# A softmax streamed through SBUF: late loads in two large tiles, first load on another queue, and one multiply per tile

## The chip, the cores and the metric

The kernel runs on one core of one Trainium2 chip. The metric is device time in microseconds, the median of repeated runs. Lower is better.

## The reference

```python
def reference(x):                 # x: 16 x 1024 x 512, float32
    temp = 2.0
    x_scaled = x / temp
    x_max = np.max(x_scaled, axis=-1, keepdims=True)
    exp_x = np.exp(x_scaled - x_max)
    return exp_x / np.sum(exp_x, axis=-1, keepdims=True)
```

It is a softmax over the last axis with temperature 2. There are 16,384 independent rows of 512 floats; input and output are 33.55 MB each.

## The kernel before

The 16,384 rows are spread over 128 partitions, so that each partition has 128 rows. Below, "a row" means one such row on all 128 partitions: 512 floats by 128 partitions, 262,144 bytes. `PLAN` cuts the 128 rows into tiles; a tile is one load and one store. Each entry holds the tile's chunks (rows per chunk) and the tile's first place in `arena`, an SBUF tensor with room for 100 rows per partition. The tiles have 3, 7, seven times 15, 7, 3 and 3 rows. Everything is done in place in the arena: load, maximum, exponential, multiply, store.

The first eight tiles (0 to 7) fill the 100 rows. Tiles 8 to 11 are late loads: each goes to a place that an earlier tile used, and so has to wait until the stores of those tiles (`behind`) have finished. `AFTER` says after which tile's exponentials ScalarE comes to that wait: late loads are issued from ScalarE's own queue between its exponentials (L133 to L137), so everything behind them on ScalarE waits too.

For each chunk there are four steps:

- VectorE takes the negated maximum of each row with one instruction for the chunk (`do_max`, L100), once the tile's load semaphore `ld` has arrived.
- ScalarE takes the exponential row by row with the maximum as bias, scale 0.5, and sums each row as it goes (L139).
- VectorE takes the reciprocal of the chunk's sums (L109).
- VectorE multiplies the chunk by its reciprocals (`do_mul`). In tiles named in `FUSED` this is one tensor_mul of the whole chunk with the reciprocals broadcast along the row (L113); in all others it is one tensor_scalar_mul for each row (L120).

VectorE's order is written out: the maximum of chunk k, then the multiply of chunk k - `LAG`, with `LAG` = 2. SyncE waits for a tile's last multiply and issues its store (L161). All loads are issued from ScalarE's queue, the first two (`issue_loads(0, 2)`) ahead of a barrier at the start of the program, the others behind it. The second load (`SPREAD`) is issued in three pieces: all rows but one, then the last row over 126 partitions and over 2 partitions. GpSimd waits for all stores at the end.

Of the kernel before, what the change touches and what calls it, by code (L numbers as in the profile page):

```python
# [8 lines left out]


PLAN = [
    ([3], 0), ([4, 3], 3), ([5] * 3, 10), ([5] * 3, 25), ([5] * 3, 40), ([5] * 3, 55),
    ([5] * 3, 70), ([5] * 3, 85), ([5] * 3, 10), ([4, 3], 3), ([3], 0), ([3], 25),
]
ARENA = 100
LAG = 2

AFTER = {8: 4, 9: 4, 10: 4, 11: 6}

SPREAD = 1  # L20

FUSED = {1, 2, 3}


@with_exitstack
def kernel(
    ctx: ExitStack,
    tc: tile.TileContext,
    x: bass.AP,
    out: bass.AP,  # L30
):
    nc = tc.nc
    fp32 = mybir.dt.float32

    xf = x.flatten_outer_dims()
    of = out.flatten_outer_dims()
    N, D = xf.shape
    P = nc.NUM_PARTITIONS
    n_rows = N // P
    assert sum(sum(c) for c, _ in PLAN) == n_rows  # L40

    arena = nc.alloc_sbuf_tensor("arena", (P, ARENA, D), fp32)
    negmax = nc.alloc_sbuf_tensor("negmax", (P, n_rows), fp32)
    sums = nc.alloc_sbuf_tensor("sums", (P, n_rows), fp32)
    recip = nc.alloc_sbuf_tensor("recip", (P, n_rows), fp32)

    tiles, chunks, base = [], [], 0
    for t, (cs, at) in enumerate(PLAN):  # L50
        r = sum(cs)
        tiles.append((base, r, at))
        o = 0
        for c in cs:
            chunks.append((t, base + o, c, at + o))
            o += c
        base += r
    last_chunk = {c[0]: k for k, c in enumerate(chunks)}

    def dram(ap, t):  # L60
        b, r, _ = tiles[t]
        return ap[b * P : (b + r) * P].rearrange("(p r) d -> p r d", r=r)

    def sb(t):
        _, r, at = tiles[t]
        return arena[:, at : at + r, :]


    behind = {}
    for t, (_, r, at) in enumerate(tiles):  # L70
        for u in range(t):
            _, ru, au = tiles[u]
            if at < au + ru and au < at + r:
                behind.setdefault(t, []).append(u)

    ld = [tc.alloc_semaphore(f"ld{t}") for t in range(len(tiles))]
    awaited = sorted({u for us in behind.values() for u in us})
    st = {t: tc.alloc_semaphore(f"st{t}") for t in awaited}
    s_end = tc.alloc_semaphore("s_end")
    s_max = tc.alloc_semaphore("s_max")  # L80
    s_exp = tc.alloc_semaphore("s_exp")
    s_rec = tc.alloc_semaphore("s_rec")
    s_mul = tc.alloc_semaphore("s_mul")

    def issue_loads(begin, end):

        for t in range(begin, end):
            if t == SPREAD:

                r = tiles[t][1] - 1  # L90
                for p, q, lo, hi in ((0, P, 0, r), (0, 126, r, r + 1), (126, P, r, r + 1)):
                    nc.scalar.dma_start(
                        out=sb(t)[p:q, lo:hi], in_=dram(xf, t)[p:q, lo:hi]
                    ).then_inc(ld[t], 16)
            elif t not in behind:
                nc.scalar.dma_start(out=sb(t), in_=dram(xf, t)).then_inc(ld[t], 16)

    def do_max(k):
        t, b, c, a = chunks[k]
        nc.vector.reduce_max(  # L100
            out=negmax[:, b : b + c],
            in_=arena[:, a : a + c],
            axis=mybir.AxisListType.X,
            negate=True,
        )._wait_ge(ld[t], 48 if t == SPREAD else 16).then_inc(s_max, 1)

    def do_mul(k):
        t, b, c, a = chunks[k]
        nc.vector.reciprocal(  # L109
            out=recip[:, b : b + c], in_=sums[:, b : b + c]  # L110
        )._wait_ge(s_exp, k + 1).then_inc(s_rec, 1)
        if t in FUSED:
            nc.vector.tensor_mul(  # L113
                out=arena[:, a : a + c],
                in0=arena[:, a : a + c],
                in1=recip[:, b : b + c].unsqueeze(2).to_broadcast([P, c, D]),
            )._wait_ge(s_rec, k + 1).then_inc(s_mul, 1)
            return
        for r in range(c):
            ins = nc.vector.tensor_scalar_mul(  # L120
                out=arena[:, a + r],
                in0=arena[:, a + r],
                scalar1=recip[:, b + r : b + r + 1],
            )
            if r == 0:
                ins._wait_ge(s_rec, k + 1)
        ins.then_inc(s_mul, 1)

    def compute_and_store():

        late = sorted(behind)
        for k, (t, b, c, a) in enumerate(chunks):
            while late and last_chunk[AFTER[late[0]]] < k:  # L133
                u = late.pop(0)
                for v in behind[u]:
                    nc.scalar.wait_ge(st[v], 16)
                nc.scalar.dma_start(out=sb(u), in_=dram(xf, u)).then_inc(ld[u], 16)  # L137
            for r in range(c):
                ins = nc.scalar.activation(  # L139
                    out=arena[:, a + r],  # L140
                    in_=arena[:, a + r],
                    func=mybir.ActivationFunctionType.Exp,
                    bias=negmax[:, b + r : b + r + 1],
                    scale=0.5,
                    accum_out=sums[:, b + r : b + r + 1],
                )
                if r == 0:
                    ins._wait_ge(s_max, k + 1)
            ins.then_inc(s_exp, 1)


        for k in range(len(chunks) + LAG):
            if k < len(chunks):
                do_max(k)
            if k >= LAG:
                do_mul(k - LAG)


        for t in range(len(tiles)):
            nc.sync.wait_ge(s_mul, last_chunk[t] + 1)  # L160
            nc.sync.dma_start(out=dram(of, t), in_=sb(t)).then_inc(  # L161
                st[t] if t in awaited else s_end, 16
            )

        for t in awaited:
            nc.gpsimd.wait_ge(st[t], 16)
        nc.gpsimd.wait_ge(s_end, 16 * (len(tiles) - len(awaited)))

    hook = nc.inst_callbacks[-1]
    nc.remove_inst_callback(hook)
    symbolic = nc._always_lower_symbolic_ap
    nc._always_lower_symbolic_ap = False
    here = str(nc.cur_bb)
    entry = nc.main_func.blocks[0]
    head, jumps = entry.instructions[:-5], entry.instructions[-5:]
    entry.instructions = []
    nc.switch_bb("main", None)
    issue_loads(0, 2)  # L180
    first = list(entry.instructions)
    at = next(k for k, i in enumerate(head) if type(i).__name__ == "InstDrain")
    entry.instructions = head[:at] + first + head[at:]
    issue_loads(2, len(tiles))
    compute_and_store()
    entry.instructions = list(entry.instructions) + jumps
    nc.switch_bb(here, None)
    nc._always_lower_symbolic_ap = symbolic
    nc.push_inst_callback(hook)
# [30 lines left out]
```

## Time and profile before

| | |
|---|---|
| median of 19 runs | 162.03 us (161.86 to 162.18) |
| the profiled execution | 161.86 us |
| its span in the profile | 160.1 us |
| VectorE (DVE) busy | 131.8 us, 155 instructions |
| ScalarE (ACT) busy | 94.6 us, 257 instructions |
| bytes moved by DMA | 67.14 MB, 419 GB/s over the span |
| maximum, line L100 | 28 instructions, 72.3 us |
| multiply by rows, L120 | 91 instructions, 37.8 us |
| multiply by chunks, L113 | 8 instructions, 21.0 us |

The span reaches from the first instruction to the last DMA packet; the time of an execution has 1.8 us more. In the groups of instructions each row names line, engine, operation, operands with their shapes, and count; behind the first bar stand the busy time in microseconds and the mean of one in nanoseconds, behind the second the idle time of the engine just before them and what ended it. In lines of the timeline the first number is the start and the second the duration, both in microseconds. "q1" is the DMA queue of SyncE and "q10" that of ScalarE in the packet records; each of the 16 DMA engines serves both.

### The profile page before, as it was taken

To read this page: it belongs to the slowest core of one execution; us is meant where nothing else is said; L and a number is where in the kernel's file an instruction comes from. 1 tells how busy PE (TensorE), PEld (TensorE's weight loads), DVE (VectorE), ACT (ScalarE), POOL (GpSimd) and SP (SyncE) were. 2 spreads that over 40 slices of the span, in tenths; PEclk is the share of its full clock that TensorE was granted. 3 is DMA by queue.
4 is the path that set the end of the run, shared out by engine and by line. 5 is a ranking of instruction groups with operands and counts; after the bars stand their busy time and mean duration, and the time that the engine had idled before them with its cause. 6 is when DMAs were issued, how large, how long until landed. Compare 5 with 4: busy or idle time off the path is not lost.

```text
span 160.1 us, 482 instructions
## 1 busy us (share of the span) xinstructions
DVE 131.8 (82%) x155; ACT 94.6 (59%) x257; POOL 0.2 (0%) x4
## 2 busy tenths in 40 slices
DVE  0466499999999999999999999999999999506800
ACT  0629266768449547766688666786667975501300
POOL 0000000000000000000000000000000000000000
DMA  7998999999998989898989999998999999999894
GB/s 279 444 407 384 424 434 421 433 474 376 425 480 384 476 384 484 376 484 378 476 384 476 407 468 422 432 468 380 454 418 451 419 396 431 431 448 468 375 418 204
DMA packets 3603, 67.14 MB, mean 419 GB/s; under 512 B 400, under 2 KB 400, under 8 KB 1296
## 3 DMA queue, kind: packets, MB, share of 16 engines
q10 hardware_dynamic: 1872, 33.56, 49.6%
q1 hardware_dynamic: 1728, 33.56, 48.8%
q14 instruction: 3, 0.02, 0.0%
HBM read 33.55 MB, written 33.55 MB: 419 GB/s over the span
## 4 chain that ended last, share of the span: by engine, by line
DVE 78%; DMA 10%; another core or an unknown queue 5%; issue 0%; DVEq 0%
DVE negmax L100 40%; DVE arena L120 23%; DVE arena L113 13%; DMA arena<-in_x_dram 10%; DVE recip L109 2%; DVEq L215 0%
## 5 line engine op out<-in xcount | busy, mean ns | idle before, releaser
L139 ACT ACTIVATE arena<-arena,negmax 128x512 f32<-128x512 f32 x128 | 90.8, 710 | 49.6 <-DVE negmax L100 49.6
L100 DVE TENSOR_REDUCE negmax<-arena 128x5 f32<-128x2560 f32 (+2 forms) x28 | 72.3, 2585 | 18.7 <-DMA arena<-in_x_dram 18.7
L120 DVE TENSOR_SCALAR arena<-arena,recip 128x512 f32<-128x512 f32 x91 | 37.8, 482 | 0.7
L139 ACT ACTIVATION_READ_ACCUMULATOR arena<-arena,negmax 128x1 f32 x128 | 23.9, 187 | 0.0
L113 DVE TENSOR_TENSOR arena<-arena,recip 128x2560 f32<-128x2560 f32 (+2 forms) x8 | 21.0, 2625 | 0.3
L109 DVE RECIPROCAL recip<-sums 128x5 f32<-128x5 f32 (+2 forms) x28 | 4.9, 176 | 0.0
L139 ACT ACT_TABLE_LOAD x1 | 1.3, 1283 | 5.4 <-issue 5.4
L204 POOL MEMSET const-bfloat16-1.0<- 128x1 bf16 x1 | 0.1, 103 | 0.0
L204 POOL MEMSET const-uint8-127<- 128x1 uint8 x1 | 0.1, 102 | 0.0
L204 POOL MEMSET const-float32-0.0<- 128x1 f32 x1 | 0.1, 100 | 0.2 <-issue 0.2
L204 POOL MEMSET const-float32-1.0<- 128x1 f32 x1 | 0.1, 99 | 0.0
## 6 DMA issues: line engine op xcount, KB each, us to landing
arena<-in_x_dram ACTq DMA_DIRECT2D x7, 3840.0 KB, 42.7
out_dram<-arena SPq DMA_DIRECT2D x7, 3840.0 KB, 23.4
out_dram<-arena SPq DMA_DIRECT2D x2, 1792.0 KB, 12.4
arena<-in_x_dram ACTq DMA_DIRECT2D x3, 768.0 KB, 50.8
out_dram<-arena SPq DMA_DIRECT2D x3, 768.0 KB, 7.5
arena<-in_x_dram ACTq DMA_DIRECT2D x1, 1792.0 KB, 55.6
arena<-in_x_dram ACTq DMA_DIRECT2D x1, 1536.0 KB
arena<-in_x_dram ACTq DMA_DIRECT2D x1, 252.0 KB
```

The costliest lines, as they stand in the source:

```text
L100: nc.vector.reduce_max(out=negmax[:, b : b + c], in_=arena[:, a : a + c], axis=mybir.AxisListType.X, negate=True,)._wait_ge(ld[t], 48 if t ...
L109: nc.vector.reciprocal(out=recip[:, b : b + c], in_=sums[:, b : b + c])._wait_ge(s_exp, k + 1).then_inc(s_rec, 1)
L113: nc.vector.tensor_mul(out=arena[:, a : a + c], in0=arena[:, a : a + c], in1=recip[:, b : b + c].unsqueeze(2).to_broadcast([P, c, D]),)._w ...
L120: ins = nc.vector.tensor_scalar_mul(out=arena[:, a + r], in0=arena[:, a + r], scalar1=recip[:, b + r : b + r + 1],)
L139: ins = nc.scalar.activation(out=arena[:, a + r], in_=arena[:, a + r], func=mybir.ActivationFunctionType.Exp, bias=negmax[:, b + r : b + r ...
L204: nc = _bacc.Bacc("TRN2", target_bir_lowering=False, num_devices=1)
```

## The change

There are now ten tiles instead of twelve: 3, 7, seven times 15, and 13 rows. `PLAN` has a new middle entry, the groups in which a tile is multiplied and stored. A tile of 15 rows has its maxima taken in chunks of 8 and 7 and is multiplied and stored as one group of 15. The late loads are tile 8 (15 rows, at place 0, behind tiles 0, 1 and 2) and tile 9 (13 rows, at place 15, behind tiles 2 and 3); tile 9 has chunks of 5, 4 and 4 and groups of 9 and 4. The first load is issued from SyncE (`FIRST`). Every multiply is one tensor_mul over its group. A group is multiplied once the maxima of the two chunks after its last chunk have been issued, so VectorE's order becomes: the two maxima of tile t, then reciprocal and multiply of tile t - 1. The second load's three pieces are in both kernels. The constants `SPREAD`, `LAG`, `FIRST` and `AFTER` appear twice with the same values.

```diff
 PLAN = [
-    ([3], 0), ([4, 3], 3), ([5] * 3, 10), ([5] * 3, 25), ([5] * 3, 40), ([5] * 3, 55),
-    ([5] * 3, 70), ([5] * 3, 85), ([5] * 3, 10), ([4, 3], 3), ([3], 0), ([3], 25),
+    ([3], [3], 0), ([4, 3], [7], 3), ([8, 7], [15], 10), ([8, 7], [15], 25),
+    ([8, 7], [15], 40), ([8, 7], [15], 55), ([8, 7], [15], 70), ([8, 7], [15], 85),
+    ([8, 7], [15], 0), ([5, 4, 4], [9, 4], 15),
 ]
...
-AFTER = {8: 4, 9: 4, 10: 4, 11: 6}
+FIRST = 1
+AFTER = {8: 4, 9: 6}
...
         for t in range(begin, end):
+            if t in behind:
+                continue
+            queue = nc.sync if t < FIRST else nc.scalar
             if t == SPREAD:
                 r = tiles[t][1] - 1
-                for p, q, lo, hi in ((0, P, 0, r), (0, 126, r, r + 1), (126, P, r, r + 1)):
...
+                parts = (0, P, 0, r), (0, 126, r, r + 1), (126, P, r, r + 1)
+            else:
+                parts = ((0, P, 0, tiles[t][1]),)
+            for p, q, lo, hi in parts:
+                queue.dma_start(
+                    out=sb(t)[p:q, lo:hi], in_=dram(xf, t)[p:q, lo:hi]
+                ).then_inc(ld[t], 16)
...
-    def do_mul(k):
-        t, b, c, a = chunks[k]
+    def do_mul(j):
+        t, b, c, a, k = groups[j]
         nc.vector.reciprocal(
             out=recip[:, b : b + c], in_=sums[:, b : b + c]
-        )._wait_ge(s_exp, k + 1).then_inc(s_rec, 1)
-        if t in FUSED:
...
-        for r in range(c):
-            ins = nc.vector.tensor_scalar_mul(
...
+        )._wait_ge(s_exp, k).then_inc(s_rec, 1)
+        nc.vector.tensor_mul(
+            out=arena[:, a : a + c],
+            in0=arena[:, a : a + c],
+            in1=recip[:, b : b + c].unsqueeze(2).to_broadcast([P, c, D]),
+        )._wait_ge(s_rec, j + 1).then_inc(s_mul, 1)
...
                 for v in behind[u]:
-                    nc.scalar.wait_ge(st[v], 16)
+                    nc.scalar.wait_ge(st[v], 16 * len(PLAN[v][1]))
...
+        j = 0
         for k in range(len(chunks) + LAG):
             if k < len(chunks):
                 do_max(k)
-            if k >= LAG:
-                do_mul(k - LAG)
+            while j < len(groups) and groups[j][4] + LAG <= k + 1:
+                do_mul(j)
+                j += 1
...
-        for t in range(len(tiles)):
-            nc.sync.wait_ge(s_mul, last_chunk[t] + 1)
-            nc.sync.dma_start(out=dram(of, t), in_=sb(t)).then_inc(
+        for j, (t, b, c, a, _) in enumerate(groups):
+            o = b - tiles[t][0]
+            nc.sync.wait_ge(s_mul, j + 1)
+            nc.sync.dma_start(out=dram(of, t)[:, o : o + c], in_=arena[:, a : a + c]).then_inc(
```

## The prediction

> **What bounds the kernel now.** I read the busy times and the 40 slices of the page first, then the DMA windows, then the groups of instructions by form, and last the order of time on VectorE around the end.
>
> ```profile
> span 160.1 us, 482 instructions
> ...
> DVE 131.8 (82%) x155; ACT 94.6 (59%) x257; POOL 0.2 (0%) x4
> ...
> DVE  0466499999999999999999999999999999506800
> ...
> DMA  7998999999998989898989999998999999999894
> ...
> DMA packets 3603, 67.14 MB, mean 419 GB/s; under 512 B 400, under 2 KB 400, under 8 KB 1296
> ```
>
> The DMA row has no slice below 7 before the last. In four windows (time, length, busy of each engine, DMA share, GB/s) the share is at 1 from start to end:
>
> ```profile
> 2.00:20.00 18.00, 8.68 (x8) 8.55 (x21) 0.00 (x0) 1.00 1.02 420
> 20.00:60.00 40.00, 39.72 (x24) 26.06 (x71) 0.00 (x0) 1.00 1.01 429
> 60.00:100.00 40.00, 39.72 (x53) 28.92 (x81) 0.00 (x0) 1.00 1.00 433
> 100.00:142.00 42.00, 37.83 (x60) 28.80 (x80) 0.00 (x0) 1.00 1.01 435
> ```
>
> So the DMA engines set the end: 67.1 MB at about 432 GB/s. One row of all 128 partitions is 262,144 bytes, hence **0.607 us a row**; 128 rows go in and 128 out. The trace's packet records give the edges: first packet at 2.59, last data at 160.09, which is the span. But VectorE has no pause between 18.4 and 138.1 us either: it follows closely behind. Its forms:
>
> ```profile
> L100 DVE TENSOR_REDUCE negmax<-arena 128x5 f32<-128x2560 f32 x21 | 59.1, 2813 | 3.6 <-DMA arena<-in_x_dram 3.6
> L120 DVE TENSOR_SCALAR arena<-arena,recip 128x512 f32<-128x512 f32 x91 | 37.8, 482 | 0.7
> L113 DVE TENSOR_TENSOR arena<-arena,recip 128x2560 f32<-128x2560 f32 x6 | 16.9, 2825 | 0.2
> ```
>
> The last multiply of tile 8 (15 rows) decides below. It ends at 134.66 (132.59 + 2.07):
>
> ```profile
> 130.71 1.75 DVE L100 TENSOR_REDUCE negmax<-arena 128x3 f32<-128x1536 f32 x1
> 132.37 0.18 DVE L109 RECIPROCAL recip<-sums 128x5 f32<-128x5 f32 x1
> 132.59 2.07 DVE L120 TENSOR_SCALAR arena<-arena,recip 128x512 f32<-128x512 f32 x5
> ```
>
> That tile's store sends its first packet only at 141.78, because earlier stores fill the queue. This 7.1 us is the lead VectorE has over the DMA engines before the end.
>
> [...] five rows take 2.07 us as five tensor_scalars, 2.825 as one tensor_tensor; a maximum of five takes 2.81. [...] the late 3-row loads (6,144-byte packets) beside 15-row stores (30,720 bytes) need 10.6 us for 3 rows, while a 15-row load beside a 15-row store needs 17.7. [...]
>
> **The change part by part.**
>
> *Durations.* A maximum of n rows, with the next instruction's start taken off, costs n x 0.533 + 0.065 (5 rows: 2.73 in the chain). A fused multiply costs n x 0.533 + 0.155 (5 rows: 2.82). A reciprocal with its wait costs 0.12. Longer instructions are on this line by extrapolation: max of 8 is 4.33, of 7 is 3.80, multiply of 15 is 8.155, of 9 is 4.955, of 7 is 3.89, of 4 is 2.29.
>
> *First load on SyncE.* It and load 1 now start together and alternate: eight packets per engine of 0.23 and 0.46 us, so load 0 lands near 8.3 and not 4.5. The first maximum ends near 10.0, the two of tile 1 near 14.0, the 3-row multiply (1.76 fused, before 1.28) near 15.9. All this hides behind load 2, which ends the next wait of VectorE at 18.38. The bytes ahead of load 2 are the same, so 18.4 stays; two queues may smooth the start, where the DMA engines move 102, 262 and 374 GB/s in the first three half microseconds, by up to 0.5. The ACT queue issues one DMA less (0.4 us), before a barrier that releases at 2.4: nothing. Load 1's three pieces, 126 and 2 partitions among them, stand in both kernels: nothing.
>
> *VectorE from 18.4 on.* In the new order one tile's maxima come before the whole multiply of the tile ahead:
> - tile 2's maxima 8.13, then tile 1's reciprocal and 7-row multiply 4.01: 30.5;
> - six rounds (maxima of tiles 3 to 8, multiplies of 2 to 7), each 4.33 + 3.80 + 0.12 + 8.155 = 16.41: 129.0;
> - maxima of 5 and 4 rows of tile 9, 4.93; tile 8's reciprocal and multiply, 8.28: **142.2**;
> - maximum of 4 rows 2.20, multiply of 9 with reciprocal 5.08: 149.5; multiply of 4, 2.41: 151.9.
>
> So tile 8 is multiplied 7.5 us later than before (134.66). Five tiles (4 to 8) cost 16.41 and not 14.79 each, +8.1; tiles 1 to 3, fused already, save 1.5 with fewer instructions; 9 rows and not 7 of late maxima stand ahead of that multiply, +1.1. It sums to 7.7, near enough.
>
> *Do other waits enter?* Loads: t3 lands near 29.5 (needed at 30.5, the closest), t4 to t7 landed at 42, 56, 74 and 92 before (needed at 46.9, 63.3, 79.8, 96.2), t8 at 110 (needed at 112.6). Tile 9 comes with 26,624-byte packets, nearly an even share beside stores: 13 rows in about 17 us, landing near 125 (needed at 129.0). ScalarE: 15 exponentials take 10.6 (0.71 each), and a tile's sums are asked for about 20 us after its first maxima. ScalarE's queue waits for the stores of tiles 0 to 2 before load 8, until about 69, and the exponentials of tile 5 stand behind that wait from about 68: 1 to 2 us late, with some 9 us of cover before their sums are needed. Load 9 waits for store 3 (about 87); ScalarE arrives there only at about 95, and the load queue has work until about 107. GpSimd waits only at the end.
>
> *The DMA engines then run dry.* When tile 8's store can be issued, everything but 28 rows (15 + 9 + 4) has been issued before. In the kernel before, 28 rows were left at 142.5 by the packet records. With the engines busy until there, they have nothing left at 142.5, while the store is issued at 142.2. The delay from issue to first packet on an idle queue: the trace shows it once, load 0, issued at 0.14, first packet at 2.59, **2.45**. Stores 0 to 2, issued beside 30,720-byte load packets, took 5.0[...]. Take away three such packets of 1.14 and 1.6 is left. I take 2.45, with 1.6 and 5.0 as ends. First packet: 142.2 + 2.45 = 144.7, a **gap of 2.2 us** in an otherwise full DMA row. Then 28 rows at 0.607 = 17.0, and about 0.4 for the last of 16 engines (they started up to 0.5 apart in the first load): 162.1. Stores of 9 and 4 rows, ready at 149.5 and 151.9 plus 2.5, find the queue busy until 153.8: hidden.
>
> *Sum.* Span 160.1 + 2.0 = 162.1. Around the span lie 161.86 - 160.08 = 1.8, giving 163.9; the median of the runs is 0.17 above the profiled execution: **164.0**. The larger late loads bring tile 9 in some 20 us sooner than the last rows before (145.5), and that buys nothing: the end hangs on the store of tile 8.
>
> **The rivals.**
> 1. *The gap is closed by a quick start of the store.* For: store latency is known only loosely, and at 1.6 the span is 142.2 + 1.6 + 17.0 + 0.2 = 161.0. With load 2 landing 0.5 sooner, 160.5. Against: load 0's 2.45. Time 162.0 to 162.9.
> 2. *Faster: the DMA engines stay the bound and gain.* Two queues at the start smooth up to 0.5, and 13 + 13 rows of small packets (6,144 bytes in 0.234 against 30,720 in 1.138, 3% less rate) return 0.2: span 159.4, 161.3 us. It decides only if tile 8's store is ready before 142.5 - 0.7 - 2.45 = 139.3, 2.9 us earlier than my chain; every duration in it is steady (2812 median, 2819 most), so this needs a cheaper long instruction than the line says.
> 3. *A longer gap.* If an idle queue too takes 5.0, the gap is 4.7 and the time 166.5. For: three stores show 5.0. Against: each had load packets ahead of it.
> 4. *A load wait on VectorE.* If t3 lands 1 us late, or load 8 or 9 is held by its stores, the chain slips by as much, one for one: 165.
>
> **How the numbers follow.** A measurement can tell about 0.2% (0.3 us). The gap as forecast, 1.6 to 3.5 of delay: 0.72, 162.8 to 165.0. Rival 1 down to no change: 0.06. Rival 2: 0.05. Rivals 3 and 4: 0.17. The range takes the main case and half of rivals 3 and 4: 162.6 to 165.6. Faster 0.05, same 0.06, slower 0.89.
>
> **What would show it.** Right: VectorE without a pause from 18.4 to near 152; a 15-row multiply of 8.1 to 8.2 us; its last of 15 rows ending near 142; a dip in the DMA row near 143 to 145, and none before. Wrong: no dip (then the end is the DMA engines' alone, and near 160), a VectorE wait on a load between 30 and 130, or a store that starts within 1 us of its issue.

## The result and the profile after

The changed kernel takes 163.82 us (median of 7 runs, 163.78 to 164.03) where the kernel before takes 162.05: a ratio of **1.0111, 95% interval 1.0102 to 1.0120**. The forecast was 164.0. The profiled execution has a span of 162.0 us, 1.9 more than before. Five of the variants below also had executions of 167 to 170 us (11 of 55 in all, while the kernel before and the changed one had none); the ratios leave these out, and two variants were traced in such an execution only, so that no lines of theirs are shown.

The rows of the page that answer to those shown of before, engine shares, slices and DMA:

```profile
span 162.0 us, 366 instructions
...
DVE 141.3 (87%) x42; ACT 92.8 (57%) x257; POOL 0.2 (0%) x4
...
DVE  0476599999999999999999999999999999999500
...
DMA  7989999999999899898989989899989989588996
...
DMA packets 3170, 67.13 MB, mean 414 GB/s; under 512 B 352, under 2 KB 352, under 8 KB 736
```

VectorE works 9.5 us longer with 42 instructions instead of 155. In the DMA row a 5 stands near the end, the only slice below 7 ahead of the last one: the dip. VectorE no longer has the low slices there, because it does not wait for a late load any more. The windows (start and end, length, busy of VectorE, ScalarE and GpSimd, clock, DMA share, GB/s) put the dip on the clock:

```profile
20.00:60.00 40.00, 39.90 (x12) 30.21 (x85) 0.00 (x0) 1.00 1.00 427
60.00:100.00 40.00, 39.93 (x10) 23.24 (x66) 0.00 (x0) 1.00 1.02 440
100.00:138.00 38.00, 37.90 (x12) 27.46 (x77) 0.00 (x0) 1.00 0.99 428
138.00:141.00 3.00, 3.00 (x1) 0.39 (x2) 0.00 (x0) 1.00 0.79 338
141.00:143.00 2.00, 2.00 (x2) 0.00 (x0) 0.00 (x0) 1.00 0.00 0
143.00:160.00 17.00, 9.09 (x5) 2.94 (x8) 0.00 (x0) 1.00 0.99 424
```

A window counts a packet where it starts, so 0 between 141 and 143 means that no packet began there. Up to 138 us the DMA engines are as full as before, 427 to 440 GB/s; then they run out of work one after the other. What VectorE does at that time, from its timeline (start, duration):

```profile
121.01 8.16 DVE L136 TENSOR_TENSOR arena<-arena,recip 128x7680 f32<-128x7680 f32 x1
129.09 5.00 DVE L124 TENSOR_REDUCE negmax<-arena 128x5 f32<-128x2560 f32 x2
134.01 0.24 DVE L133 RECIPROCAL recip<-sums 128x15 f32<-128x15 f32 x1
134.28 8.16 DVE L136 TENSOR_TENSOR arena<-arena,recip 128x7680 f32<-128x7680 f32 x1
142.36 2.28 DVE L124 TENSOR_REDUCE negmax<-arena 128x4 f32<-128x2048 f32 x1
```

The fourth line is the multiply of tile 8. It ends at 142.44; SyncE issues the store at 142.47, and in the packet records its first packet stands at 143.30. The last packet of everything issued earlier ends at 141.70, and 15 of the 16 engines are free from about 141.0. In the timelines, a row with x2 takes two instructions together and names the shape of the first.

The costs by form (busy, mean ns, idle before):

```profile
L136 DVE TENSOR_TENSOR arena<-arena,recip 128x7680 f32<-128x7680 f32 x7 | 57.1, 8159 | 0.2
L124 DVE TENSOR_REDUCE negmax<-arena 128x8 f32<-128x4096 f32 x7 | 30.9, 4415 | 3.1 <-DMA arena<-in_x_dram 3.1
...
L133 DVE RECIPROCAL recip<-sums 128x15 f32<-128x15 f32 x7 | 1.7, 241 | 0.0
```

The 3.1 us of idle time is the wait for load 2 at the start. No later load makes VectorE wait: the idle times of all its other forms on loads belong to the first two tiles.

### The profile page after: what moved, and what is told of

The parts are those of the page before. It is cut to its first block, busy times and chain, and to the rows that moved or that the text cites. A ratio compares the mean times of both kernels' runs of the same rounds, so it can differ in the third digit from the quotient of the medians.

```text
span 162.0 us, 366 instructions
## 1 busy us (share of the span) xinstructions
DVE 141.3 (87%) x42; ACT 92.8 (57%) x257; POOL 0.2 (0%) x4
## 4 chain that ended last, share of the span: by engine, by line
DVE 83%; DMA 10%; issue 0%
DVE arena L136 42%; DVE negmax L124 40%; DMA arena<-in_x_dram 10%; DVE recip L133 1%
## 5 line engine op out<-in xcount | busy, mean ns | idle before, releaser
L124 DVE TENSOR_REDUCE negmax<-arena 128x8 f32<-128x4096 f32 (+4 forms) x20 | 70.4, 3559 | 10.5 <-DMA arena<-in_x_dram 10.5
L136 DVE TENSOR_TENSOR arena<-arena,recip 128x7680 f32<-128x7680 f32 (+4 forms) x11 | 70.0, 6364 | 0.4
L133 DVE RECIPROCAL recip<-sums 128x15 f32<-128x15 f32 (+4 forms) x11 | 2.4, 220 | 0.0
```

Of the source, the lines that this page charges most:

```text
L124: nc.vector.reduce_max(out=negmax[:, b : b + c], in_=arena[:, a : a + c], axis=mybir.AxisListType.X, negate=True,)._wait_ge(ld[t], 48 if t ...
L133: nc.vector.reciprocal(out=recip[:, b : b + c], in_=sums[:, b : b + c])._wait_ge(s_exp, k).then_inc(s_rec, 1)
L136: nc.vector.tensor_mul(out=arena[:, a : a + c], in0=arena[:, a : a + c], in1=recip[:, b : b + c].unsqueeze(2).to_broadcast([P, c, D]),)._w ...
```

## The experiments

Theory 1 is the one of the prediction: VectorE's unbroken chain up to the multiply of tile 8 is too long, the DMA engines run dry, and the end comes later by what they stand idle. Theory 2 says that the new sizes of loads, stores and packets cost the DMA engines rate. Theory 3 says that the end hangs on the last multiplies, those of tile 9. Times are medians; ratios are against runs of the kernel before on the same chip.

**Longer delay.** Diff:

```diff
-    ([8, 7], [15], 0), ([5, 4, 4], [9, 4], 15),
+    ([8, 7], [15], 0), ([5, 8], [5, 8], 15),
```

> Edit: the late tile 9 has chunks and groups of 5 and 8 rows instead of chunks 5, 4, 4 and groups 9, 4. Eight rows of maxima, not four, stand between the first late maximum and the multiply of tile 8 on VectorE: 4 x 0.533 = 2.1 us more. Theory 1 (the DMA engines run dry and wait for the store of tile 8): that multiply ends at about 144.6 instead of 142.4, the gap in the DMA row grows from 2.4 to about 4.5 us, and the time goes from 163.8 to about 165.9. Theory 2 (larger packets or the even turns of loads and stores cost the DMA engines rate, and the place of the store does not matter): 163.8. Theory 3 (the end hangs on the last multiplies of tile 9, which end at about 152 in both): 163.8 to 164.2.

Measured: 165.90 us, ratio 1.0235 (1.0222 to 1.0248). Its timeline on VectorE:

```profile
129.14 7.13 DVE L124 TENSOR_REDUCE negmax<-arena 128x5 f32<-128x2560 f32 x2
136.20 0.24 DVE L133 RECIPROCAL recip<-sums 128x15 f32<-128x15 f32 x1
136.47 8.16 DVE L136 TENSOR_TENSOR arena<-arena,recip 128x7680 f32<-128x7680 f32 x1
...
147.73 4.42 DVE L136 TENSOR_TENSOR arena<-arena,recip 128x4096 f32<-128x4096 f32 x1
```

The maxima of the late tile take 7.13 instead of 5.00, the multiply of tile 8 ends 2.19 later (144.63), and the kernel is 2.08 slower. The last multiply ends at 152.15, exactly where it ended before the edit (149.87 + 2.29 = 152.16), so theory 3 falls: same last multiply, 2.1 us more. Theory 2 falls as the whole explanation: the loads and their packets are the same, and of the stores only the last two differ in size.

**Tile 8 stored in two halves.** Diff:

```diff
-    ([8, 7], [15], 0), ([5, 4, 4], [9, 4], 15),
+    ([8, 7], [8, 7], 0), ([5, 4, 4], [9, 4], 15),
```

> Edit: tile 8 is multiplied and stored in two groups of 8 and 7 rows, the rest as changed. The first 8 rows are multiplied right after the first maximum of tile 9 and end near 136.5, so their store is there before the DMA engines run dry (140.8). Theory 1: the gap of 2.4 us before tile 8 goes, but the 9-row multiply of tile 9 ends near 150.1, its store sends from about 151.0, and the DMA engines are done with the rest at 149.9: a new gap of about 1.1 us. Time about 162.6. Theory 2: 163.8, as nothing changes in what is moved but one store in two. Theory 3: 164.1, since the last multiply ends 0.3 later.

Measured: 162.35 us, ratio 1.0011 (1.0004 to 1.0018). Of the timeline:

```profile
132.25 4.42 DVE L136 TENSOR_TENSOR arena<-arena,recip 128x4096 f32<-128x4096 f32 x1
...
145.25 4.96 DVE L136 TENSOR_TENSOR arena<-arena,recip 128x4608 f32<-128x4608 f32 x1
```

The first half is multiplied by 136.67, its store has its first packet at 140.52, and the dip at 141 is gone. As forecast, a smaller one opens before the 9-row store: its multiply ends at 150.21, the first packet is at 151.06, and the DMA engines had finished the rest between 149.6 and 150.65. One edit to one group takes back 1.5 of the 1.8 us.

**Tile 9 in three groups too.** Diff:

```diff
-    ([8, 7], [15], 0), ([5, 4, 4], [9, 4], 15),
+    ([8, 7], [8, 7], 0), ([5, 4, 4], [5, 4, 4], 15),
```

> Edit: tile 8 in groups of 8 and 7, and tile 9 in groups of 5, 4 and 4, each multiplied and stored on its own. Theory 1: 5 rows of tile 9 are multiplied by about 148.0 and sent from 148.8, before the rest is done at 149.9, so no gap is left at either place; the last packet comes 2.3 us sooner than in the changed kernel, for about 161.5, 0.3% faster than before. Theory 2: 163.8 or a little more for the smaller packets of the stores. Theory 3: about 164.3, the last multiply being 0.5 later.

Measured: 161.71 us, ratio 0.9975 (0.9965 to 0.9985). It is faster than the kernel before with more instructions on VectorE than the changed kernel has, which neither rival allows. That both gaps are closed is concluded from the time; no timeline shows it.

**Cheaper multiplies.** The diff in `do_mul` of the changed kernel, shortened (the tensor_mul is the one of before, moved under the `if`):

```diff
+        if t < 4:
+            nc.vector.tensor_mul(...)._wait_ge(s_rec, j + 1).then_inc(s_mul, 1)
+            return
+        for r in range(c):
+            ins = nc.vector.tensor_scalar_mul(
+                out=arena[:, a + r], in0=arena[:, a + r],
+                scalar1=recip[:, b + r : b + r + 1])
+            if r == 0:
+                ins._wait_ge(s_rec, j + 1)
+        ins.then_inc(s_mul, 1)
```

> Edit: tiles 4 to 9 are multiplied row by row with tensor_scalar_mul again (six microseconds for 15 rows, not 8.16), all else as changed: loads, tiles, chunks, groups, stores. Theory 1: five tiles save 1.9 us each until the multiply of tile 8; VectorE then catches up with the last load (landing 126 to 128) and waits for it, and tile 8's multiply ends near 139, its store sends before the DMA engines run dry at 140.8: no gap, about 161.5. Theory 2 (loads and stores as they are in the changed kernel cost the rate): 163.8. Theory 3: the last multiply ends at about 147 instead of 152, so 4 to 5 us less would be allowed, down to what the DMA engines need, also about 161.5.

Measured: 161.59 us, ratio 0.9968 (0.9956 to 0.9980), the lowest median of all, though not apart from the three groups by its interval. Its slices show no dip, and VectorE waits for the last load:

```profile
DMA  7999999999998989899999999999999898999994
```

```profile
124.96 5.01 DVE L124 TENSOR_REDUCE negmax<-arena 128x5 f32<-128x2560 f32 x2 [2.49 <-DMA arena<-in_x_dram]
129.89 0.24 DVE L133 RECIPROCAL recip<-sums 128x15 f32<-128x15 f32 x1
130.16 6.03 DVE L144 TENSOR_SCALAR arena<-arena,recip 128x512 f32<-128x512 f32 x15
```

VectorE now waits for both late loads, 1.47 us for load 8 and 2.49 for load 9. Load 9 is there at 124.96, sooner than the 126 to 128 of the forecast, so that tile 8's multiply ends at 136.19 and not near 139. Its store has its first packet at 140.43, while the queue is still full.

Fifteen rows as fifteen instructions take 6.03 us, as one instruction 8.16. All else of the change is in this kernel (tiles, late loads, first load on SyncE, whole-tile groups), so none of that costs time by itself. Together with the three groups of the run before, it shows that two things are needed for the loss: the dearer form of the multiply, and late stores that wait for large groups of it. Either one taken away is enough; splitting tile 8 alone leaves 0.3 us of the loss.

**The multiply's form alone, in the kernel before.** Diff:

```diff
-FUSED = {1, 2, 3}
+FUSED = set(range(12))
```

> Edit to the kernel before: every chunk is multiplied with one tensor_mul (FUSED names all tiles), loads, tiles and stores as before. Fifteen chunks of tiles 4 to 8 cost 2.82 instead of 2.07 each, 11.3 us in all up to the last multiply of tile 8, which then ends at 146.0 and not at 134.7. Theory 1: the DMA engines run dry near 141, the store of tile 8 sends at 146.8, and 28 rows after it give a span of about 165.5, a time of 167.4. Theory 2 (the multiply's form does not matter because the kernel is bound by the DMA engines, the loss in the changed kernel comes from its tiles): 162.1.

Measured: 167.49 us, ratio 1.0332 (1.0318 to 1.0346). Of its slices and its timeline:

```profile
DMA  7989999999999899899899999999999999059996
```

```profile
143.10 2.82 DVE L113 TENSOR_TENSOR arena<-arena,recip 128x2560 f32<-128x2560 f32 x1
```

The last multiply of tile 8 ends at 145.92, and a slice of 4 us stands empty in the DMA row. The time is the forecast one (167.4). The fused form alone costs 5.4 us in the kernel before; the changed kernel is 3.7 faster than this one, and its multiply of tile 8 ends 3.48 sooner. Most of that is in the sums of the two timelines: a 15-row tile takes VectorE 16.48 us in the changed kernel and 17.05 here, seven such tiles make 4.0, the earlier start on load 2 (18.08 against 18.33) gives 0.3, and two more rows of late maxima take 1.1 away. No run separates these terms.

**Another order on VectorE.** Diff:

```diff
-            while j < len(groups) and groups[j][4] + LAG <= k + 1:
+            while j < len(groups) and groups[j][4] + (1 if j == 8 else LAG) <= k + 1:
```

> Edit: only the order on VectorE: the whole multiply of tile 8 comes after one late maximum (5 rows) instead of two (9 rows). Theory 1: that multiply ends at 140.3 instead of 142.4, its store sends at 141.1, the gap there shrinks from 2.3 to about 0.4; but the maxima of the second and third late chunk now come after it, the 9-row multiply of tile 9 has to wait for their exponentials and ends at 150.5, so that a second gap of about 1 us opens before its store. About 162.7. Theory 2 (rate of the DMA engines, not the place of the stores): 163.8.

Measured: 162.98 us, ratio 1.0049 (1.0035 to 1.0062). Of its timeline:

```profile
132.06 8.16 DVE L136 TENSOR_TENSOR arena<-arena,recip 128x7680 f32<-128x7680 f32 x1
140.13 4.47 DVE L124 TENSOR_REDUCE negmax<-arena 128x4 f32<-128x2048 f32 x2
145.41 0.21 DVE L133 RECIPROCAL recip<-sums 128x9 f32<-128x9 f32 x1 [0.81 <-ACT arena L152]
145.66 4.96 DVE L136 TENSOR_TENSOR arena<-arena,recip 128x4608 f32<-128x4608 f32 x1
```

The first gap nearly closes (store 8 sends at 141.08), and the new wait for ScalarE (0.81) and the second gap (150.69 to 151.48) are those forecast. The time is 0.3 above the forecast of 162.7, which lies inside the interval (162.6 to 163.1 us). This order closes most of one gap and opens another: the mean idle time of the DMA engines falls from 2.6 to 1.6 us, not to zero.

**First load back on ScalarE's queue.** Diff: `FIRST = 1` becomes `FIRST = 0`.

> Edit: FIRST = 0, so the first load goes back to ScalarE's queue; all else as changed. Theory 1 (VectorE's unbroken chain from the landing of load 2 to the multiply of tile 8 sets the end): load 2 lands at 18.4 as in the kernel before and not at 18.1, the whole chain and the end slip by 0.3, for 164.1. Rival (the queue of the first load only saves issue time that nobody waits for): 163.8.

Measured: 164.06 us, ratio 1.0118 (1.0102 to 1.0133). The first maximum of tile 2 starts later than in the changed kernel (18.08):

```profile
18.39 4.42 DVE L124 TENSOR_REDUCE negmax<-arena 128x8 f32<-128x4096 f32 x1 [3.08 <-DMA arena<-in_x_dram]
```

The multiply of tile 8 ends at 142.75, 0.3 later too. The slip along the chain is in the trace; the times alone (0.24 apart, the intervals of the ratios overlapping) would not settle it. That the slip comes from the queue of the first load is not shown: the kernel with tile 8 in halves and the row-by-row kernel have that load on SyncE and start at 18.29 and 18.34.

**Both: row-by-row multiplies, first load on ScalarE's queue.**

> Edit: row-by-row multiplies in tiles 4 to 9 and FIRST = 0 together. Here the DMA engines have no gap and set the end. If the earlier first packet on SyncE's queue (0.99 instead of 1.15, load 2 landing 0.3 sooner) is what the row-by-row version gains on the kernel before, this gives 161.8 to 161.9 and not 161.6; if the gain comes from the larger late tiles and their packets alone, 161.6.

Measured: 161.74 us, ratio 0.9980 (0.9972 to 0.9989), between the two forecasts, its interval overlapping that of the row-by-row kernel. How much of the 0.5 us by which that one beats the kernel before is the start, how much the packets, and whether anything else of the change has a part in it, **stays open**.

One table holds it together. "Idle" is the mean idle time of a DMA engine between 138 and 157 us in the packet records of the traced execution.

| kernel | tile 8 multiplied at, us | idle, us | time, us | time less idle |
|---|---|---|---|---|
| before | 134.66 | 0.0 | 162.05 | 162.0 |
| changed | 142.44 | 2.6 | 163.82 | 161.2 |
| late tile in 5 and 8 | 144.63 | 4.8 | 165.90 | 161.1 |
| tile 8 in halves | 136.67 and 142.90 | 1.3 | 162.35 | 161.1 |
| tile 8 before second late maximum | 140.22 | 1.6 | 162.98 | 161.4 |
| rows in tiles 4 to 9 | 136.19 | 0.0 | 161.59 | 161.6 |
| first load on ScalarE's queue | 142.75 | 2.6 | 164.06 | 161.5 |
| before, all fused | 145.92 | 5.7 | 167.49 | 161.8 |

The idle time explains times from 161.6 to 167.5 to within half a microsecond; what is left over differs by 0.9 at most, and no run explains that rest.

## Why the prediction was right

**VectorE's chain.** Forecast end of tile 8's multiply 142.2, measured 142.44. Two small misses partly cancel. Load 2 let VectorE start at 18.08, not 18.38. The first packet is at 0.99, before at 1.15, and load 1 is issued at 0.12, before at 0.56. With the first load on SyncE five traces have the start at 18.06 to 18.34, with it on ScalarE's queue three have 18.33 to 18.39; so the queue may bring the 0.3, but not in every trace. The prediction had allowed up to 0.5 for two queues, an estimate, and taken nothing. The reciprocal of 15 rows costs 0.19 with its wait, not 0.12, seven times over. The long instructions are on the line drawn through the short ones: 8.16 for 15 rows (forecast 8.155).

**The other waits.** None entered. ScalarE waited for store 2 until 68.9 (forecast about 69), idle for 7.4 us, and VectorE had no wait from it. Load 0 landed at 6.3, not 8.3; load 1's first packets came only about 1.4 us after its own (2.43 against 0.99), where the forecast let both start together. As was said, both stay hidden behind load 2. Load 9 took the forecast 17 us (17.01 from its first packet to its last).

**The gap.** Forecast 2.2 us; measured 1.6 with all 16 engines idle, 2.3 from the time when 15 of them were free, and 2.6 in the mean of the engines. But **the prediction read packets on a wrong clock**. It took the end of the last packet for the end of the span, as the note under the table ahead of it does. In the trace of the kernel before, the last packet ends at 158.65 and the span at 160.08: every packet time in the prediction stands 1.43 too late against the instructions. The first packet was at 1.15, not 2.59, and the first load's delay 1.01, not 2.45. The stores beside load packets took 3.5 to 3.6, not 5.0. The 28 rows were left at about 141.1, not 142.5. Tile 8's store had its first packet at 140.34, not 141.78, so VectorE's lead was 5.7 us and not 7.1.

In the sum the error drops out: the queue's end and the store's first packet were both set 1.4 too late, and the 1.3 us between the last packet and the end of the span (162.00 less 160.68) were left out. What is then left is partly luck. The store was issued 0.27 later than forecast. Its delay was 0.83, which is 2.15 when the packets are set 1.32 later, as that clock would do here, and so 0.30 shorter than the forecast 2.45. The two misses cancel. On the right clock the sum reads: issue 142.47, first packet 143.30, 28 rows and the last engine 17.38 (forecast 17.0 + 0.4), 1.32 to the end: 162.0.

**The signs.** Of those for "right", VectorE's unbroken chain (18.08 to 152.16), the 15-row multiply of 8.16 and its end at 142.44 are in the trace; the dip came at 141.0 to 143.3 and not near 143 to 145, which is the error of the clock again. Of those for "wrong", "a store that starts within 1 us of its issue" came true, and the mechanism holds all the same, since the experiments show it and the sign was set on the shifted clock.

**The rivals.** A start of the store in 1.6 on the prediction's clock (rival 1) did not come: there it is 2.15. A longer delay on an idle queue (rival 3) did not show. The faster case (rival 2) needed tile 8's multiply 2.9 us sooner. The row-by-row kernel supplied that, and the kernel with three groups has half of tile 8 ready early (136.67 in the kernel that groups tile 8 alike); they took 161.59 and 161.71, near the 161.3 it named. So that case is real where its condition is met, while which of its two sources pays is open, as said above. No load wait (rival 4) came.

## What to carry to other kernels

When transfers are the bound, an engine close behind them may be slowed only by the lead it has: here 5.7 us between a multiply's end and the first packet of its store, of which a store on idle DMA engines takes some 0.85 itself. Ask of every merged instruction not what it saves in count but when the store behind it can start, and how many bytes stand queued at that moment. Cutting the last groups smaller, or choosing the form of the multiply that took less time here (15 rows in 6.03 us, not 8.16), brought the changed kernel from 1.1% slower to 0.3% faster than before.

## What the runs showed of the hardware

- A store issued on idle DMA engines has its first packet 0.83 us after the start of the issuing instruction (142.47 to 143.30), which takes 0.33 of that; in the six traces with such a store it is 0.85 to 0.86 after the end of the multiply (142.44 to 143.30 in the changed kernel, 150.21 to 151.06 with tile 8 in halves). Beside 30,720-byte load packets it was 3.5 to 3.6 here, some 2.4 packets of 1.14 more; what such a store waits for is not shown.
- While loads and stores are both under way, about as many packets of the one queue start as of the other, at each of the sizes here. In the kernel before, the 128 packets of a late 3-row load (6,144 bytes) go beside 127 store packets of 30,720 bytes and take 10.57 us; those of a 15-row load (30,720 bytes) beside 125, in 17.6. In the changed kernel those of load 9 (26,624 bytes) go beside 130. One queue alone has 16 packets in progress at once (ScalarE's at 10 us, SyncE's at 150).
- The span ends 1.3 to 1.4 us after the last data packet (160.68 against 162.00, 158.65 against 160.08). Packet records and instructions must be set on one clock by their own time stamps, not by their ends.
- A reciprocal of 15 values per partition takes 241 ns, of 3 values 168: some 6 ns for each further value. The tensor_mul takes 1.04 for each further value (8,159 ns for 7,680, 2,825 for 2,560).
- The last sixteen 4-byte packets of the kernel before end between 157.85 and 158.65, those of the changed kernel, which has the gap, between 160.45 and 160.68. The records do not name the DMA engine; a gap may hide such a lag, and so "time less idle" be lowest in kernels with gaps. That was not tested.
